# Reordering the streamed weight blocks of a hybrid decoder block on one core

## The chip, the core and the metric

The kernel runs on one core of a Trainium2 chip. Its engines have queues of their own and meet through semaphores: TensorE (PE, with its weight loads shown as PEld), VectorE (DVE), ScalarE (ACT), GpSimd (POOL) and SyncE (SP), which here issues most of the DMAs. The metric is the device time of one execution in microseconds (us), the median of several runs.

## The reference

A decoder block for 256 tokens of width 2048, batch 1, in f32. The input is RMS-normalised and multiplied by one wide matrix `w_in` (2048 x 8760), whose columns feed everything that follows:

- an mLSTM with 4 heads of 256: `mq`, `mk` (through a causal convolution of 4 taps and SiLU), `mv`, the output gate `mo`, the path gate `mz`, input and forget gates `mi`, `mf`;
- native sparse attention with 16 query heads of 64 in 4 key/value groups: queries `nq`, three pairs of keys and values (`kc`,`vc` compressed, `ks`,`vs` selected, `kw`,`vw` windowed), three mixing gates `ng` and a path gate `nz`. The compressed keys and values each go through a small two-layer network with GELU over blocks of 32 tokens.

```python
m_out = hm * jax.nn.sigmoid(mo) * jax.nn.silu(mz)
n_out = n_att * jax.nn.silu(nz)
x = x + jnp.concatenate([m_out, n_out], axis=-1) @ w_out[l]
ple = rmsnorm(p[l] @ ple_proj_w[l], ple_norm_g[l])
x = x + jax.nn.sigmoid(x @ ple_gate_w[l]) * ple
```

A last RMSNorm gives the output.

## The kernel before

All weights are streamed once, in the order of the list `STREAM` (lines 54 to 65). Each entry is a block of columns, cut along the contraction into 216 **units** of mostly 512 KB. Products are made to nearly full f32 precision from rounded parts: ACT rounds a unit to `whi` (L164), DVE takes the remainder `wlo` (L165), and PE multiplies hi by hi, hi by lo and lo by hi. Token-major blocks do this in `mm` at L190 (stationary x, moving weights, two token halves of 128 in two PSUM banks); blocks marked `feat` (the convolved `qk0` to `qk7` and the gates `nz0` to `nz3`) have the weights stationary (L178, L179). Four buffers hold raw, hi and lo units; main results rotate through three PSUM banks (`mainps`), the small transposes through two (`auxps`).

The main loop (L1273 and on) takes one unit per turn, in this order: evacuate the block that ended in the turn before (`evac`, the functions `ev_*`); issue the load of the unit four ahead and the split of the unit three ahead; issue this unit's matmuls; then `advance()`, which runs every **track** by one step. A track is a Python generator: what stands between two `yield`s is issued in one turn, behind that turn's matmuls on PE and behind its split on ACT and DVE. All engines execute in the order of issue. So the place of a step in time is counted in units, and a wait in a step holds all that is queued behind it on its engine.

The tracks that matter here, with their lines:

- `x_squares` (L260) loads x in 8 pieces into `xq`, squares them, and `norm_scale` (L272) makes the token scales `rr` (a power on POOL, L275), `rh`, `rq` and, through PE (L281), the row `rb`. It starts at unit 4.
- `split_w1` (L476) splits the two 1 MB first layers of the compressions; `k_stack` (L364) turns rope'd keys into `kT`.
- `compress` (L485): `cmp_hidden` (L392) for the keys, then for the values. Each is a chain of 14 steps: transposes, copies `kcs`, windows `mov` on POOL, split `movr`, PE matmuls (L430), GELU, second layer. Both use one buffer for `movr`.
- `nsa` (L578): query transposes, scores against the compressed keys, then `cmp_probs` (L624, a softmax over them) beside `attend_all` (L659): 12 sub-steps of four turns each: scores (L670), mask and maximum on DVE (L680, L682), exponentials on ACT (L693), scaling on POOL (L704), transposes on PE (L716), split (L727, L728), product with the values (L740 to L749). It waits for `cmp`, and `attend_all` also for the window keys (`k1`) and the gates (`vw`).
- `conv` (L867): convolution and SiLU of a `qk` block on DVE and ACT (L875 to L882).
- `mlstm` (L903): four heads, three turns each, after `nsa`, `gates` and `conv7`; then normalisation to `hm`.
- `gate_m` (L1012) and `gate_n` (L1050) multiply by the gates and make the hi/lo inputs `mixm`, `mixn` of the output projection; `ple_in` and `ev_ple` make the per-layer embedding.

Blocks before: `cs` (units 0 to 15), `kw`, `vw` (16 to 27), `q0` to `q2` (28 to 51), `qk0` to `qk7` (52 to 83), `mv` (84 to 99), `mo` (100 to 115), `mz` (116 to 131), four times `nz`, `ple` (132 to 151), `out` (152 to 183), `gate` (184 to 215).

## Time and profile before

| | |
|---|---|
| median of 3 runs | 672.66 us (670.83 to 674.17) |
| the profiled execution | 671.72 us, of which the trace spans 670.0 us |
| busy | PE 647.0 us (97%), DVE 456.4 (68%), ACT 376.4 (56%), POOL 73.7 (11%) |
| TensorE's mean granted clock | 0.991 of full speed |
| DMA | 121.05 MB, 181 GB/s on the mean |

Times of the trace count from the span's start. Matmuls are pipelined, and a PE that is shown busy need not be at its peak; here the number of matmuls in a stretch says how far the work got. In the timelines the first number is the start in us, the second the duration; in brackets stands how long the engine was idle before and what ended it.

### The profile page before, as it was taken

To read this page: it belongs to the slowest core of one execution; us is meant where nothing else is said; L and a number is where in the kernel's file an instruction comes from. 1 tells how busy PE (TensorE), PEld (TensorE's weight loads), DVE (VectorE), ACT (ScalarE), POOL (GpSimd) and SP (SyncE) were. 2 spreads that over 40 slices of the span, in tenths; PEclk is the share of its full clock that TensorE was granted. 3 is DMA by queue.
4 is the path that set the end of the run, shared out by engine and by line. 5 is a ranking of instruction groups with operands and counts; after the bars stand their busy time and mean duration, and the time that the engine had idled before them with its cause. 6 is when DMAs were issued, how large, how long until landed. Compare 5 with 4: busy or idle time off the path is not lost. (4 is left out here: it accounts for less than half of the span.)

```text
span 670.0 us, 9336 instructions
## 1 busy us (share of the span) xinstructions
PE 647.0 (97%) x3423; PEld 557.0 (83%) x3423; DVE 456.4 (68%) x682; ACT 376.4 (56%) x643; POOL 73.7 (11%) x78
## 2 busy tenths in 40 slices
PE   8999999999979999999999999997999999999994
PEld 6888999988968888888888888876888888888884
DVE  5667848788789999766675556676645755545564
ACT  5577756477457775665656444566744433445442
POOL 0002303000030112111211000110100000022430
PEclk9999999999999999999999999998999999999998
DMA  8993756565444545555455554453687765566623
GB/s 288 371 355 100 201 167 173 175 198 180 129 121 131 157 156 158 159 157 157 144 164 154 184 155 139 142 149 112 195 297 267 252 183 183 190 184 192 186 97 127
DMA packets 36479, 121.05 MB, mean 181 GB/s; under 512 B 4305, under 2 KB 5073, under 8 KB 35921
## 3 DMA queue, kind: packets, MB, share of 16 engines
q1 hardware_dynamic: 35280, 115.98, 54.7%
q10 hardware_dynamic: 1152, 4.47, 1.8%
q8 instruction: 27, 0.44, 0.3%
q14 instruction: 20, 0.16, 0.1%
HBM read 118.33 MB, written 2.10 MB: 180 GB/s over the span
## 5 line engine op out<-in xcount | busy, mean ns | idle before, releaser
L165 DVE TENSOR_TENSOR wlo<-wraw,whi 128x1024 fp32r<-128x1024 f32 (+3 forms) x218 | 260.3, 1196 | 175.9 <-ACT whi L164 170.2
L164 ACT CAST whi<-wraw 128x1024 fp32r<-128x1024 f32 (+3 forms) x218 | 217.0, 998 | 189.6 <-PE mainps L190 120.9
L190 PE MATMUL mainps<-whi,hT 128*128 128x512 f32 (+3 forms) x768 | 184.0, 360 | 0.9 <-ACT whi L164 0.8
L190 PEld LDWEIGHTS mainps<-whi,hT 128*128 128x128 f32 x768 | 131.7, 189 | 18.1 <-ACT whi L164 1.6
L178 PE MATMUL mainps<-hT,whi 128*128 128x512 f32 x384 | 139.3, 404 | 3.3 <-ACT ple L1091 1.5
L179 PE MATMUL mainps<-hT,wlo 128*128 128x256 f32 x384 | 108.1, 282 | 0.0
L190 PE MATMUL mainps<-wlo,hT 128*128 128x512 f32 (+3 forms) x384 | 106.5, 356 | 0.1
L178 PEld LDWEIGHTS mainps<-hT,whi 128*128 128x128 f32 x384 | 72.9, 190 | 20.7 <-ACT ple L1091 1.8
L190 PEld LDWEIGHTS mainps<-wlo,hT 128*128 128x128 f32 x384 | 68.3, 188 | 9.4 <-DVE wlo L165 0.5
L179 PEld LDWEIGHTS mainps<-hT,wlo 128*128 128x128 f32 x384 | 73.3, 191 | 0.3
L190 PE MATMUL mainps<-whi,x2T 128*128 128x512 f32 (+1 forms) x288 | 70.4, 366 | 0.0
L190 PEld LDWEIGHTS mainps<-whi,x2T 128*128 128x128 f32 x288 | 50.8, 189 | 8.8
L190 PE MATMUL mainps<-wlo,x2T 128*128 128x512 f32 (+1 forms) x144 | 40.9, 366 | 0.0
L704 POOL TENSOR_TENSOR pr<-pr,st 128x1024 f32<-128x1024 f32 x12 | 23.0, 1913 | 143.5 <-DVE st L702 93.3
L190 PE MATMUL mainps<-whi,mixm 128*128 128x512 f32 x128 | 35.5, 399 | 0.0
L190 PE MATMUL mainps<-whi,mixn 128*128 128x512 f32 x128 | 34.2, 389 | 0.0
L878 DVE SCALAR_TENSOR_TENSOR qk<-cv,csb,qk 128x253 f32<-128x253 f32 (+2 forms) x48 | 29.5, 614 | 1.6 <-ACT qk L875 0.2
L190 PEld LDWEIGHTS mainps<-wlo,x2T 128*128 128x128 f32 x144 | 26.0, 189 | 4.4
L190 PEld LDWEIGHTS mainps<-whi,mixn 128*128 128x128 f32 x128 | 24.0, 188 | 5.1
L190 PEld LDWEIGHTS mainps<-whi,mixm 128*128 128x128 f32 x128 | 23.6, 188 | 5.2
L693 ACT ACTIVATE pr<-wideps,st 128x128 f32<-128x128 f32 (+1 forms) x64 | 26.3, 423 | 2.7 <-DVE st L682 2.7
L1191 POOL TENSOR_TENSOR x<-x,gth 128x512 f32<-128x512 f32 x6 | 11.3, 1881 | 117.5 <-PE mainps L190 102.5
(276 smaller groups left out, 711.3 us busy)
## 6 DMA issues: line engine op xcount, KB each, us to landing
wraw<-in_wst_dram SPq DMA_DIRECT2D x183, 512.0 KB, 3.6
wraw<-in_wst_dram SPq DMA_DIRECT2D x24, 344.0 KB, 3.2
wraw<-in_wst_dram SPq DMA_DIRECT2D x8, 304.0 KB, 3.1
xq<-in_x_dram SPq DMA_DIRECT2D x8, 256.0 KB, 9.0
w1raw<-in_w_dram SPq DMA_DIRECT2D x2, 1024.0 KB, 9.9
x<-in_x_dram ACTq DMA_DIRECT2D x4, 512.0 KB, 4.8
out_dram<-x SPq DMA_DIRECT2D x8, 256.0 KB, 2.6
xf<-in_xT_dram SPq DMA_DIRECT2D x3, 512.0 KB, 6.1
```

The costliest lines, as they stand in the source:

```text
L164: A.copy(hi[:, a:z], raw[:, a:z])
L165: V.tensor_tensor(lo[:, a:z], raw[:, a:z], hi[:, a:z].bitcast(F32), OP.subtract)
L178: PE.matmul(o, wh, b.xT(kt, True), start=kt == 0, stop=False, skip_group_check=True)
L179: PE.matmul(o[:, 0], wl, b.xT(kt)[0], start=False, stop=kt == b.nk - 1, skip_group_check=True)
L190: PE.matmul(b.ps[n], xx, (self.hi, self.lo)[part == 2][:, j, a:z], start=kt + part == 0, stop=part == 2 and kt == b.nk - 1)
L693: A.activation(d["pr"][:, j, b], d["ps"][:, j, b], AF.Exp, bias=st[:, 0, j, b:b + 1], accum_out=st[:, 1, j, b:b + 1])
L704: G.tensor_tensor(pf, pf, d["st"][:, 2].rearrange("p j b -> p (j b)")[:, :, None].to_broadcast([128, 2 * jn, nk]), OP.mult)
L878: V.scalar_tensor_tensor(y[:, d:S], a[:, 0:S - d], w(j), y[:, d:S], op0=OP.mult, op1=OP.add)
L1191: G.tensor_tensor(x2[t][:, sl], x2[t][:, sl], ths[t], OP.add)
```

## The change

It reorders `STREAM` and the list of blocks alike: the three query blocks follow `cs`; then `kw`, `vw`; then `mo`, `mv`, and only then the eight convolved blocks; each `ple` block precedes its `nz` block. It lets the compression of the values start four steps behind that of the keys. It moves four POOL multiplications or subtractions to DVE, a second read of PSUM in `ev_mz` from DVE to ACT, and shifts the start of several tracks and steps.

```diff
 STREAM = [("cs", "w_in", span(C_KC, 512) + span(C_KS, 512), KT, 1)]
+STREAM += [(f"q{i}", "w_in", span(C_MI + i * 344, 344), KT, 2) for i in range(3)]
 STREAM += [("kw", "w_in", span(C_KW, 256), KT, 4), ("vw", "w_in", span(C_VW, 304), KT, 2)]
-STREAM += [(f"q{i}", "w_in", span(C_MI + i * 344, 344), KT, 2) for i in range(3)]
+STREAM += [(f"mo{i}", "w_in", span(C_MO + i * 512, 512), KT, 2) for i in range(2)]
+STREAM += [(f"mv{i}", "w_in", span(C_MV + i * 512, 512), KT, 2) for i in range(2)]
 STREAM += [(f"qk{i}", "w_in", span(C_MQ + i * 256, 256), KT, 4) for i in range(8)]
-STREAM += [(f"mv{i}", "w_in", span(C_MV + i * 512, 512), KT, 2) for i in range(2)]
-STREAM += [(f"mo{i}", "w_in", span(C_MO + i * 512, 512), KT, 2) for i in range(2)]
 STREAM += [(f"mz{i}", "w_in", span(C_MZ + i * 512, 512), KT, 2) for i in range(2)]
 for i in range(4):
+    STREAM += [(f"ple{i}", "ple_proj_w", span(i * 512, 512), 2, 2)]
     STREAM += [(f"nz{i}", "w_in", span(C_NZ + i * 256, 256), KT, 4)]
-    STREAM += [(f"ple{i}", "ple_proj_w", span(i * 512, 512), 2, 2)]
...
         V.tensor_scalar(rq, rr, ND ** -0.5, None, op0=OP.mult)
+        yield
+        yield
         ps = aux([128, S])
...
+        while is_v and "ckmm" not in done:
+            yield
         movr = tmp.tile([128, CS, 2, NG, NC16], F32R, name="movr", tag="hm")
...
+        done.add("ckmm")
...
-        yield from cmp_hidden(kcx, pkcol, w1[0], False)
-        yield
-        yield from cmp_hidden(vcx, pvcol, w1[1], True)
+        hk, hv = cmp_hidden(kcx, pkcol, w1[0], False), cmp_hidden(vcx, pvcol, w1[1], True)
+        for _ in range(4):
+            next(hk)
+            yield
+        left = [hk, hv]
+        while left:
+            for h in list(left):
+                if next(h, 1):
+                    left.remove(h)
+            yield
         done.add("cmp")
...
-        G.tensor_tensor(pcf, pcf, a0[:, :, None].to_broadcast([128, T * NH, NC16]), OP.subtract)
+        V.tensor_tensor(pcf, pcf, a0[:, :, None].to_broadcast([128, T * NH, NC16]), OP.subtract)
...
-            G.tensor_tensor(pt, pt, cmul[:, t, None, :].to_broadcast([128, NH, NC16]), OP.mult)
+            V.tensor_tensor(pt, pt, cmul[:, t, None, :].to_broadcast([128, NH, NC16]), OP.mult)
+        yield
...
-        G.tensor_tensor(pcf, pcf, a1[:, :, None].to_broadcast([128, T * NH, NC16]), OP.mult)
+        V.tensor_tensor(pcf, pcf, a1[:, :, None].to_broadcast([128, T * NH, NC16]), OP.mult)
...
             run(s_scale, k - 1)
             run(s_fin, k - 2)
             yield
+            if k == 1:
+                yield
             run(s_max, k)
             run(s_tr, k - 1)
...
         done.add(f"conv{i}")
+        if i == 7:
+            tracks.append(mlstm())
...
-            if i == 1:
-                tracks.append(mlstm())
...
-        while not {"nsa", "gates", "conv7"} <= done:
+        while not {"nsa", "gates"} <= done:
...
                 A.activation(tz, ps[t], AF.Tanh, scale=rh[:, t:t + 1])
-                V.scalar_tensor_tensor(tz, tz, 1.0, ps[t], op0=OP.add, op1=OP.mult)
+                zc = t2([128, 512], name="zc")
+                A.copy(zc, ps[t])
+                V.scalar_tensor_tensor(tz, tz, 1.0, zc, op0=OP.add, op1=OP.mult)
...
         A.activation(th, tz, AF.Tanh, scale=0.5)
+        yield
         V.scalar_tensor_tensor(tz, th, 1.0, tz, op0=OP.add, op1=OP.mult)
-        G.tensor_tensor(tz, tz, natt[:, 2 * i:2 * i + 2], OP.mult)
+        V.tensor_tensor(tz, tz, natt[:, 2 * i:2 * i + 2], OP.mult)
...
-    ple_first = next(i for i, u in enumerate(units) if u.b is mz[1])
+    ple_first = next(i for i, u in enumerate(units) if u.b is mz[0])
...
             if i == 1:
                 nc.sync.dma_start(pos_i, positions)
-            else:
                 tracks.append(x_squares())
```

The list of blocks follows the new `STREAM`: `blocks += mo + mv_b + qk_b + mz`, then `[pb[i], nz[i]]` for each i.

## Rows read from the trace of the kernel before

**Rows 1.** Busy us (instructions) of PE, PEld, DVE, ACT, POOL; then PEclk, DMA, GB/s.
```profile
14.00:51.00 37.00, 37.00 (x164) 30.59 (x163) 24.67 (x44) 25.09 (x45) 0.00 (x0) 1.00 0.97 355
51.00:54.00 3.00, 1.55 (x11) 1.14 (x10) 2.40 (x6) 0.48 (x2) 2.75 (x4) 1.00 0.74 203
...
128.00:133.00 5.00, 4.57 (x30) 4.29 (x29) 4.74 (x12) 4.00 (x8) 0.00 (x0) 1.00 0.67 197
...
180.00:210.00 30.00, 26.46 (x148) 22.90 (x147) 26.91 (x38) 18.37 (x44) 6.46 (x5) 0.94 0.39 119
210.00:262.00 52.00, 52.00 (x293) 44.70 (x292) 50.69 (x76) 36.10 (x75) 5.77 (x3) 1.00 0.48 146
262.00:358.00 96.00, 96.00 (x477) 80.72 (x476) 65.60 (x81) 58.55 (x128) 13.34 (x8) 1.00 0.51 158
...
410.00:440.00 30.00, 29.45 (x162) 25.30 (x160) 20.76 (x43) 17.58 (x30) 3.34 (x2) 1.00 0.46 141
440.00:462.00 22.00, 16.49 (x85) 13.52 (x84) 15.86 (x25) 13.54 (x27) 2.21 (x1) 0.92 0.49 143
...
661.00:670.00 9.00, 0.05 (x1) 0.00 (x0) 2.91 (x10) 1.72 (x3) 0.56 (x1) 0.71 0.63 234
sum 670.00, PE 646.96 PEld 556.99 DVE 456.35 ACT 376.42 POOL 73.66; mean PE 43.13 PEld 37.13 DVE 30.42 ACT 25.09 POOL 4.91
```

**Rows 2.** Waits of PE: waiter, released by: us in total, times, longest us.
```profile
PE auxps L1031 <- DVE mixm L1037: 3.9, 2, 3.1
PE auxps L716 <- POOL pr L704: 2.3, 1, 2.3
PE mainps L178 <- ACT ple L1091: 1.5, 1, 1.5
PE auxps L281 <- POOL rr L275: 1.4, 1, 1.4
PE mainps L178 <- ACT sc L863: 1.2, 1, 1.2
...
PE mainps L178 <- DVE tz L1005: 0.5, 1, 0.5
```

**Rows 3.** Timeline: the twelfth unit's remainder on DVE, PE's pass over it.
```profile
34.93 1.23 DVE L165 TENSOR_TENSOR wlo<-wraw,whi 128x1024 fp32r<-128x1024 f32 x1 [2.82 <-ACT whi L164]
...
38.10 0.39 PE L190 MATMUL mainps<-wlo,hT 128*128 128x512 f32 x1
```

**Rows 4.** Groups by line: DVE from 50 to 72 us, ACT from 53 to 66 us.
```profile
L481 DVE TENSOR_TENSOR w<-w1raw,w 128x512 fp32r<-128x512 f32 x8 | 5.5, 684 | 0.0
...
L507 DVE SCALAR_TENSOR_TENSOR vst<-mainps,rr,vst 128x256 fp32r<-128x256 f32 x2 | 1.0, 480 | 0.9 <-ACT vst L506 0.9
...
L515 ACT ACTIVATE kx<-mainps,rr 128x256 f32<-128x256 f32 x2 | 0.9, 475 | 1.3 <-DVE vst L507 1.3
...
L506 ACT ACTIVATE vst<-mainps,rr 128x256 fp32r<-128x256 f32 x2 | 0.9, 470 | 1.8 <-POOL rr L275 1.8
```

**Rows 5.** Timeline: POOL's first step of the compressed softmax.
```profile
186.92 1.88 POOL L631 TENSOR_TENSOR pc<-pc,cst 128x512 f32<-128x512 f32 x1 [74.93 <-DVE cst L630]
```

**Rows 6.** Timelines of POOL, DVE and PE around two scalings of the attention.
```profile
264.55 1.90 POOL L704 TENSOR_TENSOR pr<-pr,st 128x1024 f32<-128x1024 f32 x1 [11.40 <-PE mainps L190]
...
265.17 2.35 DVE L165 TENSOR_TENSOR wlo<-wraw,whi 128x1024 fp32r<-128x1024 f32 x1
...
221.73 1.90 POOL L704 TENSOR_TENSOR pr<-pr,st 128x1024 f32<-128x1024 f32 x1 [21.20 <-DVE st L702]
...
225.83 1.04 PE L716 MATMUL auxps<-ident,pr 128*128 128x128 f32 x8
```

**Rows 7.** Timeline of ACT and DVE ahead of PE's longest wait, 451 to 454 us.
```profile
451.11 0.62 ACT L1056 CAST mixn<-tz 128x512 fp32r<-128x512 f32 x1 [2.63 <-POOL tz L1054]
...
452.58 0.47 ACT L1036 ACTIVATE mixm<-auxps,csb 128x256 fp32r<-128x256 f32 x1
...
453.85 0.48 DVE L1037 SCALAR_TENSOR_TENSOR mixm<-auxps,csb,mixm 128x256 fp32r<-128x256 f32 x1
```

More of the change, by code (lines that the diff above doesn't have):

```diff
@@ L1235, in hybrid_block @@
     blocks = [Block("cs", ev_cs, h_of, cuts=halves, banks=cs_banks, parts_first=2)]
+    blocks += [Block(f"q{i}", ev_q(i), h_of) for i in range(3)]
     blocks += [Block("kw", ev_kw, h_of), Block("vw", ev_vw, h_of)]
-    blocks += [Block(f"q{i}", ev_q(i), h_of) for i in range(3)]
-    blocks += [Block(f"qk{i}", ev_qk(i), h_of, feat=True) for i in range(8)]
-    blocks += [Block(f"mv{i}", ev_mv(i), h_of) for i in range(2)]
+    mv_b = [Block(f"mv{i}", ev_mv(i), h_of) for i in range(2)]
+    qk_b = [Block(f"qk{i}", ev_qk(i), h_of, feat=True) for i in range(8)]
     pb = [Block(f"ple{i}", ev_ple(i), p_of) for i in range(4)]
@@ L1242, in hybrid_block @@
                   for c, f, n in (("mo", ev_mo, 2), ("mz", ev_mz, 2), ("nz", ev_nz, 4)))
-    blocks += mo + mz
+    blocks += mo + mv_b + qk_b + mz
     for i in range(4):
-        blocks += [nz[i], pb[i]]
+        blocks += [pb[i], nz[i]]
     blocks += [Block(f"out{i}", ev_out(i), mix_of) for i in range(4)]
```

## The prediction

> **What bounds the kernel now.** I read the table of busy times by stretch first, then the waits of PE, then the timelines around those waits. PE is busy 646.96 of 670.0 us [rows 1], and the change neither adds nor drops a matmul: 216 units before and after. So it can win only where PE idles or runs on a slow clock. Of the 23.04 us of idle time, 8.95 lie behind 661 us, after the last matmul [rows 1], and five stretches hold the rest that can move: 1.45 (51 to 54 us), 0.43 (128 to 133), 3.54 (180 to 210), 0.55 (410 to 440) and 5.51 (440 to 462), together 11.48 [rows 1]. The remaining 2.6 belong to the start, which stays. Two of these stretches also show a granted clock of 0.94 over 30 us and of 0.92 over 22 us [rows 1]: the level of 1.2 GHz instead of 2.4 for some microseconds after PE had stood still 2.3 and 3.1 us [rows 2]. That is 0.06 x 30 + 0.08 x 22 = 1.8 + 1.76 us of full-speed work. **The most that a better order can give back is 11.48 + 3.56 = 15.0 us.** The sum below is made against the profiled execution, 671.72 us, which is 0.94 below the median of 672.66 and inside the runs' spread.
>
> **The change part by part.** A step's place is counted in units by its yields; I counted both orders from the code.
>
> *Token scales.* PE waited 1.4 us for the power on POOL [rows 2]. `x_squares` now starts three units earlier and its matmul comes two steps later, so `rr` is there before it is wanted: 1.45 us go. `rb` comes later, but its first reader is 70 units away. In exchange three of the eight x pieces (3 x 256 KB = 0.79 MB) go ahead of weights in SP's queue, in a stretch where DMA is 97% busy at 355 GB/s [rows 1]: weights of units 8 to 13 land up to 2.2 us later. The tightest of them is the twelfth unit: its remainder ends at 36.16 us and PE's pass over it starts at 38.10 [rows 3], 1.94 us of slack. Loss between 0 and 2.2; I take 0.3, what the slack fails to cover.
>
> *Query blocks second.* A 512-column matmul takes 37.00 us / 164 = 226 ns [rows 1], so I estimate 152 ns for 344 columns and 0.9 us for a query unit's first token half (six matmuls). The second half needs a bank of `cs`, which the chain `vst`, its remainder, `kx` frees after 0.47 + 0.48 + 0.48 = 1.43 us [rows 4]. In the old place the first half was longer. I take 0.5 (0 to 1.5). The query units then last 1.8 us, and units 16 to 22 each carry 0.68 us of DVE for the split of the first layers [rows 4] beside the key stack, so the lead of three units shrinks: 0.4 (0 to 1.5).
>
> *Compressions overlapped.* The chain for the values starts at unit 27 instead of 37 and `cmp` is done at 41 instead of 50. It waits for the keys' `ckmm` without cost, as the keys' matmuls come at unit 30 and the values' split at 32. The attention now waits for the window keys (unit 51) and the gates (54): its first scores come at unit 55 instead of 65, it ends at 114 instead of 124. The wait of 0.43 at 128 us, DVE's end of that chain, can occur for each of two chains: 0.4 (0 to 0.9).
>
> *Compressed softmax on DVE, one step more.* POOL took 1.88 us for the first subtraction [rows 5] with ACT's exponential queued behind it and behind that the evacuation `sc` for which PE waited 1.2; then PE waited 2.3 for the first scaling L704 [rows 2]. DVE now does this in short steps, in the `mo` blocks, where there is no convolution: the stretch most like it, attention beside `mv` and `mo`, has DVE busy 65.6 of 96 us and PE idle for none [rows 1]. The extra yield gives the first scaling one more unit. The 3.54 and 1.8 go; I leave 0.3 (0 to 3.5).
>
> *Convolution under attention.* Before, half of the `qk` blocks ran beside the attention; now all eight do (units 84 to 115, attention to 113). There DVE is busy 50.69 of 52 us, 97.5%, with PE idle for 0 [rows 1]. It just holds, and must hold twice as long. A scaling ends at 223.63 us and PE transposes its result at 225.83 [rows 6], 2.2 us of slack. I take 0.7 (0 up to the second rival). A remainder that met a scaling of 1.90 us on POOL took 2.35 us, against 1.23 alone [rows 6, 3]; the 97.5% contain this already. The Trainium skill has a rule for it that speaks against this order ("SBUF — State Buffer", section "Who interferes with whom"): a DVE instruction with two SBUF inputs and a GpSimd instruction that reads SBUF shut each other out for a whole instruction. The trace agrees (2.35 beside 1.90); by that rule at its hardest, with nothing hidden, seven scalings in the convolved blocks would make the sum 7 x 1.9 = 13.3 us worse.
>
> *mLSTM and `mz`.* The mLSTM is released by the last convolution, at unit 119 instead of 124. The extra copy moves the second read of the bank to ACT, and PE no longer waits for DVE's L1005 (0.5 [rows 2]), but ACT now needs two instructions a half and still has mLSTM exponentials ahead of them: I leave 0.8 (0 to 1.5).
>
> *Gates and mixing.* PE's longest waits, 3.1 and 0.8 for `mixm` and 1.5 for the `ple` evacuation [rows 2], came when ACT stood 2.63 us behind POOL's multiplication by `natt` [rows 7] and DVE behind ACT. That multiplication goes to DVE and the step is cut in two. What stays: the four second transposes of two tracks need two banks that the first ones hold. In that unit ACT has a split (1.0) and four evacuations of 0.47, DVE 1.23 and four of 0.48 [rows 7, 3], so the first bank is free at about 1.0 + 1.1 + 1.2 + 1.0 = 4.3 us, when PE arrives at 0.9 + 2.8 = 3.7, and the second 0.5 later than wanted: 1.1. With 0.6 for the `ple` evacuation, 1.7 stay of 5.51 + 1.76 = 7.3 (0 to 7.3).
>
> *At no cost:* `mo` and `mv` earlier (evacuated by ACT alone), `ple_in` eight units earlier (an ACT-queue load with 12 units to land), and `nz3` last: its `mixn` is ready at unit 154 and first used at 159; the x loads behind it go out from 155 and are first read at 160. If one of these were late, a unit of the output projection would wait, about 3 us.
>
> **Sum:** 0.3 + 0.5 + 0.4 + 0.4 + 0.3 + 0.7 + 0.8 + 1.7 = 5.1 us stay or are new; 15.0 - 5.1 = 9.9 us are won. 671.72 - 9.9 = **661.8 us**, 1.6% below the median of before.
>
> **The rivals.** *The mixing stretch does not get better.* Both tracks still start in the same turn, and the mLSTM's own tail on DVE, POOL and ACT is unchanged; then up to 7.3 instead of 1.7 + 0.8 stay: 661.8 + 4.8 = 666.6. Against it: ACT's 2.63 us behind POOL were the head of that wait [rows 7].
> *DVE falls short in the convolved blocks.* Each of the seven scalings there costs DVE 2.35 - 1.23 = 1.12 us [rows 6, 3]. If the 2.5% of DVE that are left [rows 1] do not cover this over eight blocks, PE waits for it: 7 x 1.12 = 7.8, 669.6 us, no change that can be told. Against it: PE idles for none in 52 us of this mixture, three scalings among them [rows 1]. This is the mechanism of the rule of the Trainium skill named above ("SBUF — State Buffer").
> *Each scaling in the convolved blocks stalls PE (slower than before).* If DVE's queue delays L704 by more than the 2.2 us of slack [rows 6], PE stands before the transposes as it did at the first scaling: 2.3 us plus 1.8 of clock, for seven sub-steps 28.7, so 661.8 + 28 = 690 us. In the new order the scaling falls in the third unit of a block, away from the evacuation and the first convolution step, which speaks against it.
> *The earlier compression buys nothing* because the attention is held by keys and gates: true in part and counted; it has no price of its own.
>
> **How the numbers follow.** Forecast 0.62; mixing as before 0.20; DVE short 0.11; scalings that stall 0.07. The forecast's own range goes from all 15.0 won (656.7) to its upper ends at the front and in `mz` together (about 665). The range of 656 to 668 adds the first rival and leaves out the second, the third and strays, 2 in 10. A measurement of this kernel can tell some 0.5% from no change, 3.4 us: faster means below 669.3, which the forecast and the first rival give, and a little of the second: 0.84. Same 0.10, slower 0.06.
>
> **What would show it.** Right: no wait of PE at L281, L716 or L1031 above 1 us, a granted clock of 1.00 in every stretch behind the start, first attention scores before 150 us, the mLSTM's first matmuls some 20 us earlier (13.6 us of five units and 7 of waits), DVE above 95% in the convolved blocks with PE idle near 0. Wrong: PE waits on L716 for L704 in several blocks; PE waits for `wlo` within the first 50 us; a wait of 3 us at L1031 and a slow clock behind it; a lead that vanishes in the query units.

## The result, and the profile after

The changed kernel takes **668.31 us** (median of 11 runs, 667.21 to 670.60) against 672.66 (11 runs): ratio 0.994, interval 0.9927 to 0.9954. It is faster by 0.6%: 4.35 us where 10.9 were forecast, just outside the range of 656 to 668. Its profiled execution took 668.31 us, of which the trace spans 666.6: 3.4 less than before. Lines below about 280 keep their numbers; L281, L704, L716, L1031, L1036, L1037, L1052 of before are L283, L717, L729, L1048, L1053, L1054, L1069 now.

PE's waits in the changed kernel, to be read against [rows 2]:

```profile
PE auxps L1048 <- DVE mixm L1054: 3.0, 2, 2.5
PE auxps L383 <- DVE kst L372: 1.8, 1, 1.8
...
PE auxps L729 <- POOL pr L717: 1.3, 1, 1.3
PE mainps L190 <- ACT kx L527: 1.1, 1, 1.1
...
PE auxps L434 <- DVE movr L428: 0.5, 1, 0.5
PE mainps L190 <- ACT zc L1021: 0.3, 1, 0.3
```

Gone are POOL's `rr` (1.4), the first scaling (2.3) and the evacuation `sc` (1.2). New are the wait for the key parts `kst` (1.8), for a bank of the first block, freed by `kx` (1.1), and for one of the attention's later scalings, `pr` (1.3). The wait for `mixm` has hardly moved: 3.9 before, 3.0 now.

Busy times by stretch of the changed kernel, columns as in [rows 1]:

```profile
0.00:17.00 17.00, 13.05 (x52) 10.07 (x53) 8.18 (x25) 8.84 (x14) 0.70 (x6) 1.00 0.84 285
...
52.00:56.00 4.00, 2.87 (x17) 2.46 (x16) 2.85 (x6) 1.95 (x6) 0.00 (x0) 1.00 0.83 240
...
61.00:65.00 4.00, 2.07 (x14) 1.65 (x14) 3.96 (x8) 4.00 (x7) 0.00 (x0) 1.00 0.46 150
...
80.00:100.00 20.00, 19.54 (x135) 18.75 (x134) 16.77 (x38) 11.10 (x20) 7.36 (x14) 1.00 0.57 168
...
180.00:262.00 82.00, 82.00 (x418) 69.36 (x417) 50.72 (x66) 47.38 (x101) 11.43 (x7) 1.00 0.50 155
262.00:330.00 68.00, 68.00 (x408) 59.82 (x407) 66.00 (x100) 48.94 (x104) 7.87 (x4) 1.00 0.44 140
330.00:380.00 50.00, 48.66 (x263) 41.69 (x261) 41.77 (x63) 29.27 (x40) 2.18 (x1) 1.00 0.61 185
380.00:426.00 46.00, 45.66 (x220) 38.19 (x219) 29.04 (x57) 24.72 (x41) 2.04 (x1) 1.00 0.44 137
426.00:450.00 24.00, 20.74 (x112) 17.34 (x111) 18.16 (x27) 15.55 (x29) 0.00 (x0) 0.93 0.47 142
```

The attention's start (180 to 262 us) is full, as forecast. The idle time behind 17 us is 1.13 + 1.93 + 0.46 + 1.34 + 0.34 + 3.26 = 8.46 us, and the clock of 0.93 over 24 us (part of it at 1.2 GHz instead of 2.4) costs 1.7: 10.1 where 15.0 stood before and 4.8 were forecast (the 5.1 without the start's 0.3). The start idles 3.95 us, 1.34 more than before, which makes 15.0 - 10.1 - 1.3 = 3.6, the 3.4 of the spans. Nothing ties that 1.34 to the change: in the nine kernels below with the same code up to 80 us the start idles 1.6 to 3.3 us, on both sides of the 2.61 of before.

Two parts came out otherwise; the timelines show where. The front, ACT and VectorE:

```profile
52.44 0.47 ACT L518 ACTIVATE vst<-mainps,rr 128x256 fp32r<-128x256 f32 x1
...
54.40 0.47 ACT L527 ACTIVATE kx<-mainps,rr 128x256 f32<-128x256 f32 x1 [1.50 <-DVE vst L519]
...
57.59 0.79 ACT L164 CAST whi<-wraw 128x688 fp32r<-128x688 f32 x1
...
58.41 0.88 DVE L165 TENSOR_TENSOR wlo<-wraw,whi 128x688 fp32r<-128x688 f32 x1 [2.65 <-ACT whi L164]
...
62.79 1.22 DVE L372 TENSOR_TENSOR kst<-kx,kst 128x1024 fp32r<-128x1024 f32 x1
```

ACT empties the first block's banks from 52.44 to 57.59 us (1.50 us of it standing for VectorE's remainder `vst`, which is queued behind the remainders of two units, the row `rb` and a split piece) and rounds no unit meanwhile, so VectorE in turn stands 2.65 us; the rotation and the remainders queue behind that, and `kst` ends at 64.0 with PE waiting. The mixing:

```profile
428.07 1.29 DVE L1039 TENSOR_TENSOR hm<-hm,gmt 128x512 f32<-128x512 f32 x2
...
430.41 1.28 DVE L1039 TENSOR_TENSOR hm<-hm,gmt 128x512 f32<-128x512 f32 x2
431.60 1.03 PE L1048 MATMUL auxps<-ident,hm 128*128 128x128 f32 x8
...
433.19 0.63 ACT L1069 ACTIVATE th<-tz 128x512 f32<-128x512 f32 x1 [2.64 <-DVE tz L880]
...
437.41 0.84 ACT L1053 ACTIVATE mixm<-auxps,csb 128x256 fp32r<-128x256 f32 x2 [1.31 <-DVE mixm L1054]
...
438.55 0.99 PE L1048 MATMUL auxps<-ident,hm 128*128 128x128 f32 x4 [2.53 <-DVE mixm L1054]
```

"x2" and "x8": both halves of the mixing (one of each `mz` block) run in the same turns, and their transposes take both spare banks at once. ACT stands 2.64 us, as before, but ahead of the `tanh` (L1069), not behind a multiplication by `natt`.

### The profile page after: what moved, and what is told of

It is laid out like the page before. It is cut to its first block, busy times and chain, and to the rows that moved or that the text cites. A ratio compares the mean times of both kernels' runs of the same rounds, so it can differ in the third digit from the quotient of the medians.

```text
span 666.6 us, 9325 instructions
## 1 busy us (share of the span) xinstructions
PE 645.2 (97%) x3423; PEld 555.6 (83%) x3423; DVE 456.0 (68%) x690; ACT 378.6 (57%) x647; POOL 62.6 (9%) x70
## 4 chain that ended last, share of the span: by engine, by line
PE 84%; DVE 8%; ACT 3%; issue 2%; DMA 1%; POOL 1%; SPq 0%; ACTq 0%; POOLq 0%
PE mainps L190 56%; PE mainps L178 10%; PE mainps L179 5%; DVE wlo L165 3%; PE wideps L190 3%; PE wideps L683 2%; PE auxps L729 1%; ACT whi L164 1%; DMA wraw<-in_wst_dram 1%; PE wideps L958 1%; PE po L762 1%; PE po L760 1%; PE auxps L1185 1%; PE auxps L933 1%; PE wideps L622 1%
## 5 line engine op out<-in xcount | busy, mean ns | idle before, releaser
L178 PE MATMUL mainps<-hT,whi 128*128 128x512 f32 x384 | 137.6, 400 | 0.3 <-ACT ple L1109 0.3
L717 POOL TENSOR_TENSOR pr<-pr,st 128x1024 f32<-128x1024 f32 x12 | 23.3, 1944 | 219.1 <-DVE st L715 219.1
L878 ACT COPY sc<-mainps 128x512 f32<-128x512 f32 x24 | 14.1, 586 | 17.5 <-PE mainps L179 17.4
L893 DVE SCALAR_TENSOR_TENSOR qk<-cv,csb,qk 128x253 f32<-128x253 f32 (+2 forms) x48 | 23.1, 481 | 1.1
```

What stands on the lines that cost most here:

```text
L178: PE.matmul(o, wh, b.xT(kt, True), start=kt == 0, stop=False, skip_group_check=True)
L717: G.tensor_tensor(pf, pf, d["st"][:, 2].rearrange("p j b -> p (j b)")[:, :, None].to_broadcast([128, 2 * jn, nk]), OP.mult)
L878: A.copy(sc, ps[m])
L893: V.scalar_tensor_tensor(y[:, d:S], a[:, 0:S - d], w(j), y[:, d:S], op0=OP.mult, op1=OP.add)
```

## The experiments

Each is the changed kernel with the edit shown, unless it says otherwise. Times are medians of 5 to 12 runs; the kernel before, run beside them, had medians of 671.39 to 672.86 us, so kernels of different groups are compared by their ratios to it (with 95% intervals; they are no quotients of the medians). Two kernels whose intervals overlap can't be told apart by time. Where the order of the blocks is edited, the diff shows the list of blocks; `STREAM` follows it.

**The mixing: banks, the tanh, POOL.** `mix_gap` puts a turn between the two pairs of transposes:

```diff
                 V.scalar_tensor_tensor(lo, ps[:, j], g, hi.bitcast(F32), op0=OP.mult, op1=OP.subtract)
+            if k0 == 4 * i:
+                yield
```

> The second pair of transposes of each mixing track is put one turn behind the evacuation of the first pair. Theory A (the 2.5 us stall at the second transposes comes from taking both spare banks again in the turn in which they are still being emptied): the wait of PE at the transposes for mixm falls from 3.0 us to under 0.6, the granted clock stays near 1.0 over 428-449 us, the time falls by 3 to 4.7 us against the changed kernel, to 663.6-665.3. Rival B (ACT and VectorE are late as a whole there, because ACT stands 2.64 us at the tanh of the gate for VectorE): the stall only moves to the banks of the projection and gate blocks, the sum of PE's waits in 426-450 falls by less than 1 us, the time is within 1 us of 668.3.

666.64 us, 0.991 (0.9884 to 0.9935). The wait at the transposes fell to 0.7 (A: under 0.6) and the clock stayed 1.00, as A said; but 1.5 us came up at an evacuation of the gate blocks (L878), as B said. Half of each; by time it can't be told from the changed kernel.

`th_late` issues the gate's tanh a turn later:

```diff
+        yield
         th = t2([128, 2, S], name="th")
```

> The tanh of every gate block is issued one turn later, so that ACT is not held 2.64 us for VectorE's two additions ahead of it. Theory B (this hold of ACT is the head of the mixing wait): ACT's wait at the tanh falls from 2.64 to under 0.8 us, PE's wait at the transposes from 3.0 to about 1, the slow clock behind it goes, the time falls by 2.5 to 4 us, to 664.3-665.8. Rival A (the reuse of the two spare banks within one turn is enough by itself): ACT's wait falls all the same but PE still waits 2 us or more there, the time is within 1 us of 668.3.

667.05 us, 0.9916 (0.9887 to 0.9945), again not told from it by time. The wait fell from 3.0 to 2.3, the clock stayed slow: the hold of ACT is a part, not the head. `natt_pool` undoes one edit, VectorE's multiplication by `natt`:

```diff
-        V.tensor_tensor(tz, tz, natt[:, 2 * i:2 * i + 2], OP.mult)
+        G.tensor_tensor(tz, tz, natt[:, 2 * i:2 * i + 2], OP.mult)
```

> Of the change only one edit is undone: the multiplication of the gate by the attention output goes back from VectorE to POOL. The forecast's step (ACT's 2.63 us of waiting behind POOL's multiplication was the head of the mixing wait, and taking it off POOL saves 3 us or more): the time rises by 2.5 to 5 us, to 670.8-673.3, PE's waits in 426-450 grow by 2 us. Rival (ACT is held ahead of that, at the tanh, for VectorE, so where the multiplication runs does not matter): the time is within 1 us of 668.3.

669.27 us, 0.995 (0.9932 to 0.9968), the wait at the transposes 3.1: no difference that can be told. In the changed kernel the multiplication is not the head of the mixing wait, as the forecast had it. `mix_all` joins the first two and issues of each pair both high parts, then both low parts:

```diff
+            for j in range(2):
+                A.activation(mixm[:, 0, k0 + j], ps[:, j], AF.Copy, scale=mgcol[:, k0 + j:k0 + j + 1])
             for j in range(2):
...
-                A.activation(hi, ps[:, j], AF.Copy, scale=g)
```

> Three edits of the mixing at once: a turn between the two pairs of transposes, the tanh of the gate block one turn later, and of each pair both high parts first, then both low parts (instead of high, low, high, low, where ACT waited 1.31 and 0.58 us for VectorE's low part). Theory A+B (bank reuse and the two hold-ups of ACT are all that stalls PE here): PE's waits over 426-455 fall from 5.0 us (3.0 for mixm, the rest for evacuations) to under 1.2, granted clock 1.0; the time falls by 3.5 to 5 us, to 663.3-664.8. Rival E (each of the two engines has more work in these turns than the turns are long, so a stall left out in one place comes back at the next bank): waits of 2 us or more stay, the time is 666 to 667, as with either edit alone.

663.81 us, 0.9858 (0.9833 to 0.9884). By stretch, PE is now full where it idled 3.26 us, at full clock:

```profile
426.00:450.00 24.00, 24.00 (x137) 20.80 (x136) 20.68 (x30) 19.32 (x34) 0.00 (x0) 1.00 0.61 196
```

So the stall can be taken away there; what the order of the evacuations gives alone was not tried. Why the changed kernel runs into it, the next group shows.

**The place of the convolved blocks.** `conv_first` undoes that part of the order:

```diff
-    blocks += mo + mv_b + qk_b + mz
+    blocks += qk_b + mv_b + mo + mz
```

> Of the change one part is undone: the convolved blocks go back ahead of the values and the output gate (first block, query, key, value, convolved, values, gate). Theory F (it was this edit that freed the attention's start, by taking the convolution's multiply-adds off VectorE there): PE idles 2.5 us or more in the attention's first 60 us again and loses up to 1.8 us to a slow clock, while the single 1.3 us stall at the probabilities late in the attention goes: 670 to 672. Rival G (the query block's place and the earlier probabilities are enough, VectorE's load may lie anywhere under the attention): within 1 us of 668.3.

667.56 us, 0.9912 (0.9888 to 0.9935): the time does not tell it from the changed kernel, so G held, but not for its reason. By stretch, the attention's start idles 2.9 us again, with VectorE at 80.41 of 82, though at other waits than before: 1.8 us for `pcT` and four scalings in a row that come 0.3 to 0.6 us late each (228 to 272 us), without a slow clock. The mixing idles none:

```profile
180.00:262.00 82.00, 79.08 (x460) 68.10 (x461) 80.41 (x118) 55.51 (x118) 10.05 (x5) 1.00 0.46 148
...
426.00:450.00 24.00, 24.00 (x137) 20.70 (x136) 18.07 (x26) 17.00 (x31) 0.00 (x0) 1.00 0.54 162
```

```profile
PE auxps L729 <- POOL pr L717: 1.8, 4, 0.6
```

and in VectorE's timeline the halves of the mixing lie 13 us apart, each alone ("x1"):

```profile
416.35 0.68 DVE L1039 TENSOR_TENSOR hm<-hm,gmt 128x512 f32<-128x512 f32 x1
...
429.45 0.68 DVE L1039 TENSOR_TENSOR hm<-hm,gmt 128x512 f32<-128x512 f32 x1
```

So this part of the change moved a loss from the attention's start to the mixing; over 100 to 450 us idle time and slow clock are 4.0 us in `conv_first` and 6.6 in the changed kernel. The groups of the tiles `natt` (the attention's sums) and `em` (the mLSTM's first step of each head), with the durations (min/median/max) and the first and last start, say how. In the changed kernel, shown first, the mLSTM's first head comes 27.2 us after the attention's last sum (345.2 to 372.4), where before, shown below it, it was 14.2 (372.6 to 386.8), and in `conv_first` 14.1:

```profile
L772 DVE TENSOR_TENSOR natt<-po,ot x16: 407/414/419, 189.0 to 345.2; 64x256 f32<-64x256 f32 x16
...
L943 DVE TENSOR_TENSOR em<-auxps,mask_t x4: 417/418/418, 372.4 to 407.3; 128x256 f32<-128x256 f32 x4
```

```profile
L759 DVE TENSOR_TENSOR natt<-po,ot x16: 408/413/419, 221.5 to 372.6; 64x256 f32<-64x256 f32 x16
...
L928 DVE TENSOR_TENSOR em<-auxps,mask_t x4: 416/418/418, 386.8 to 422.3; 128x256 f32<-128x256 f32 x4
```

`conv_mixed` puts the value blocks between the convolved ones, the last convolved block staying last:

```diff
-    blocks += mo + mv_b + qk_b + mz
+    blocks += mo + qk_b[0:3] + mv_b[0:1] + qk_b[3:6] + mv_b[1:2] + qk_b[6:8] + mz
```

> The two value blocks are put between the convolved blocks (gate, gate, three convolved, value, three convolved, value, two convolved), so that the multiply-adds of the convolution spread over 83 turns' length less densely. Theory K (VectorE is short by some 0.2 us a turn while eight convolved blocks follow each other under the attention, 97% busy over 262-330 us, and the stall of 1.3 us at the probabilities is the end of that): that stall goes, PE idles under 0.3 us over 180-380, VectorE's busiest 68 us fall below 90%; 666.6 to 667.4. Rival L (the stall is one meeting of POOL's multiplication with a low part on VectorE, whatever the load): a stall of 1 us or more comes back at another probability; within 0.6 us of 668.3.

666.64 us, 0.9911 (0.988 to 0.9943). PE idles 0.06 us over 180 to 380 and VectorE's busy time over 262 to 330 falls to 60.22 of 68, as K says. The mixing's wait stays at 3.3 us, its mLSTM starting at 371.9, and by time it can't be told from the changed kernel. Then the two that settle it. `mv_last`:

```diff
-    blocks += mo + mv_b + qk_b + mz
+    blocks += mo + qk_b[0:4] + mv_b[0:1] + qk_b[4:8] + mv_b[1:2] + mz
```

> The changed kernel with the second value block moved behind the convolved blocks (gate, gate, four convolved, value, four convolved, value), so that the last convolution is over some 13 us earlier. Theory O (the mLSTM of the changed kernel starts 27 us after the attention's last sum, where 14 would do, because its own part of the change put the convolved blocks last; it then ends after the second gate block, and both halves of the mixing are released into the same turns): the mLSTM's first row moves from 372 to about 360 us, the halves' multiplications by the gate lie 8 us or more apart instead of side by side, PE's wait at the mixing's transposes (3.0 us) and the slow clock behind it go, and with the convolution thinned the 1.3 us stall at the probabilities goes as well: 662 to 664.5. Rival A' (the two spare banks are too few for a half of the mixing alone): the wait at the transposes stays 1.5 us or more: 665.5 to 667.

663.41 us, 0.9877 (0.9862 to 0.9892). PE's waits no longer list the mixing, the mLSTM's first head starts at 358.6, and in VectorE's timeline the halves are apart (the group of `em` stands below it):

```profile
411.48 0.69 DVE L1040 TENSOR_TENSOR hm<-hm,gmt 128x512 f32<-128x512 f32 x1
...
424.58 0.68 DVE L1040 TENSOR_TENSOR hm<-hm,gmt 128x512 f32<-128x512 f32 x1
```

```profile
L944 DVE TENSOR_TENSOR em<-auxps,mask_t x4: 415/417/418, 358.6 to 394.5; 128x256 f32<-128x256 f32 x4
```

One part of the expectation missed: VectorE's busy time over 262 to 330 us is as low as in `conv_mixed` (58.80 of 68), and yet PE waits for a scaling twice, 0.57 us at 265 and 0.70 at 336, each time at the third scaling beside four convolved blocks in a row (the account of the prediction says why):

```profile
PE auxps L730 <- POOL pr L718: 1.3, 2, 0.7
```

`mix_apart`:

```diff
-        while "mlstm" not in done:
+        while "mlstm" not in done or (i and "mix0" not in done):
             yield
```

> The changed kernel with one condition more: the second half of the mixing waits until the first half is done. Everything else stays, the order high, low, high, low too. Theory O: with the halves apart each takes one spare bank a turn, the wait at the transposes falls from 3.0 to under 0.6 us and the clock stays 1.00: 663.3 to 665.3. Rival A' (the hold of ACT at the tanh and the order of the evacuations stall PE even for one half): 1.5 us or more of waits stay in 426-450: 666 to 667.5.

664.36 us, 0.9884 (0.9866 to 0.9901). PE is busy 23.35 of 24 us in the mixing, at full clock, and its wait at the transposes is this:

```profile
PE auxps L1048 <- DVE hm L1039: 0.6, 1, 0.6
```

Both held in the mixing: the halves' meeting makes the stall, and in the changed kernel the place of the last convolved block makes the meeting.

`cmp_pool` puts the four operations of the compressed probabilities back on POOL:

```diff
-        V.tensor_tensor(pcf, pcf, a0[:, :, None].to_broadcast([128, T * NH, NC16]), OP.subtract)
+        G.tensor_tensor(pcf, pcf, a0[:, :, None].to_broadcast([128, T * NH, NC16]), OP.subtract)
...
```

> Of the change one part is undone: the four multiplications and subtractions of the compressed probabilities go back from VectorE to POOL. Theory H (they were part of the stall of 3.5 us and of the slow clock at the attention's start): PE idles 1 to 3 us there again, 669.3 to 672. Rival (with the gates and values ahead, the compressed probabilities have time enough on either engine): within 0.8 us of 668.3.

669.67 us, 0.9945 (0.9924 to 0.9966), and PE is busy 82.00 of 82 us at the attention's start: not told from the changed kernel. With the convolution out of the way, POOL does as well.

**The front.** `split_late` starts the split of the compression weights seven turns later, `split_early` three turns earlier with two pieces a turn, `split_mid` at turn 20 with two pieces a turn:

```diff
-        elif i == KT - 1:
-            tracks.append(split_w1(w1r))
...
+        if i == KT + 6:
+            tracks.append(split_w1(w1r))
```

(`i == 12` in `split_early`, `i == KT + 4` in `split_mid`; these two also yield only after every second piece.)

> The split of the two compression weights into high and low parts begins 7 turns later, behind the key block's evacuation. Theory C (the splits that stand in ACT's and VectorE's queues between the query block's evacuation and the key block's high and low parts hold up both): PE's wait at the transposes of the key parts falls from 1.8 to under 0.5 us, that for the query block's last bank from 1.1 to about 0.5, the time falls by 1.5 to 2.5 us, to 665.8-666.8. Rival D (ACT's evacuations of the query and key blocks and VectorE's rotation are long enough alone): the two waits together stay over 2 us, the time is within 0.8 us of 668.3.

672.08 us, 0.999 (0.9973 to 1.0007): C's two waits did go, but PE waited for the compression's moving parts instead, and the clock fell behind it (0.83 over 20 us, 3.4 us). PE's waits, and the stretch:

```profile
PE auxps L434 <- DVE movr L428: 4.1, 2, 3.6
```

```profile
80.00:100.00 20.00, 15.95 (x91) 14.77 (x90) 16.20 (x33) 9.79 (x18) 6.76 (x11) 0.83 0.45 132
```

> The split of the two compression weights begins 3 turns earlier and takes two pieces a turn, so that it is over when the first block's banks are emptied (turns 12 to 15, where VectorE was 66% and ACT 65% busy). Theory C (what the front lost is the splits standing between the evacuation of the first blocks and the key parts; the compression's tail has room only if they come no later): PE's wait for kst falls from 1.8 to under 0.6 us, the wait for the first block's bank from 1.1 to about 0.5, the wait for movr stays at 0.5, no slow clock over 61-80 us; the time falls by 2.5 to 4.5 us, to 663.8-665.8. Rival D (ACT's evacuations alone hold the key parts up, or the splits now delay the high and low parts of the first 16 turns): PE idles 1 us or more in 17-52 or the two waits stay over 2 us; 667.5 or more.

672.44 us, 0.9991 (0.9975 to 1.0007). The wait for `kst` went, that for the bank became 4.6, and the clock fell behind it (0.57 over 56 to 61 us, 0.68 over 61 to 65: 3.4 us). VectorE's free third of 17 to 52 us (23.07 of 35 us busy in the changed kernel) lies ahead of 44 us, where units come late; behind that it has no gap, and the pieces push the evacuation back. VectorE's timeline, then PE's waits:

```profile
43.70 1.23 DVE L165 TENSOR_TENSOR wlo<-wraw,whi 128x1024 fp32r<-128x1024 f32 x1 [2.45 <-ACT whi L164]
...
56.94 0.48 DVE L520 SCALAR_TENSOR_TENSOR vst<-mainps,rr,vst 128x256 fp32r<-128x256 f32 x1
```

```profile
PE mainps L190 <- ACT kx L528: 4.6, 1, 4.6
```

> The split of the two compression weights goes into turns 20 to 23, two pieces a turn: behind the first block's evacuation and behind the key parts, but ahead of the turns over 80-90 us where VectorE has no room (16.8 of 20 us busy) and where a later split delayed the compression's moving parts. Theory C' (both waits of the front come from the pieces that stand ahead of the evacuation and of the key parts, and there is one gap, 65 to 76 us, where VectorE idles 3.7 us with the pieces in it): the wait for kst falls from 1.8 to under 0.5 us, the wait for movr stays under 1, the clock stays 1.00 over 61-100; the time falls by 2 to 4 us, to 664.3-666.3. Rival D' (there is no room anywhere in the front; each place only moves the stall): the waits for kst, movr and the transposes of the compression keep a sum of 2.3 us or more; 667.5 or more.

666.17 us, 0.9903 (0.9872 to 0.9933). `kst` 1.0 instead of 1.8, `movr` 0.7, the bank still 1.1, the clock 1.00. The time is the low end of C', but its wait for `kst` (under 0.5) was missed, and its interval overlaps the changed kernel's a little.

`b_q2` is the kernel *before* with the query block second and nothing else:

```diff
 blocks = [Block("cs", ev_cs, h_of, cuts=halves, banks=cs_banks, parts_first=2)]
+blocks += [Block(f"q{i}", ev_q(i), h_of) for i in range(3)]
 blocks += [Block("kw", ev_kw, h_of), Block("vw", ev_vw, h_of)]
-blocks += [Block(f"q{i}", ev_q(i), h_of) for i in range(3)]
```

> The kernel before with one part of the change alone: the query block second. Theory M: the stall at the key parts appears (1.5 to 2.2 us), with 0.5 to 1.3 us at the first block's bank beside the wait of 1.4 us that the kernel before has there, and up to 1.6 us of slow clock; the attention still starts behind the compression and gains nothing: 673.5 to 677. Rival N: the front looks as in the kernel before, 670.5 to 673.

675.97 us, 1.0057 (1.0037 to 1.0076): slower than before. Its waits of PE hold the 1.8 for `kst` (at the line of before), and a larger one that no theory named: at 136 us the window values' banks were freed 4.9 us late, because the rotation of the queries, the key stack and this evacuation had come into the same turns of VectorE; behind it the clock was 0.96 over the 80 us from 100 on, 3.2 us:

```profile
PE mainps L178 <- DVE gates L541: 4.9, 1, 4.9
...
PE auxps L381 <- DVE kst L370: 1.8, 1, 1.8
```

`kw_q_vw` puts the window keys' four turns ahead of the query block again:

```diff
+    blocks += [Block("kw", ev_kw, h_of)]
     blocks += [Block(f"q{i}", ev_q(i), h_of) for i in range(3)]
-    blocks += [Block("kw", ev_kw, h_of), Block("vw", ev_vw, h_of)]
+    blocks += [Block("vw", ev_vw, h_of)]
```

> The changed kernel with the first key block of the window moved back ahead of the query block (first block, key, query, value, gate, values, convolved). Theory M (the front's new stalls come from the length of a turn: a query turn gives PE 1.88 us, a key turn 2.88, so the first four turns after the first block last 7.5 us instead of 11.5, and ACT's evacuations, the rotation and the splits don't fit): with the key block's four turns back, the waits for the bank and for kst fall from 1.1 and 1.8 us to under 0.5 together, the clock stays 1.00 over 56-80 us, and since the compression sets when the attention starts, nothing is lost later; 663.8 to 666. Rival N (the front's work is late because of what it is, the pieces of the split and the order of evacuation): waits of 2 us or more stay, 667.3 or more.

668.64 us, 0.9944 (0.993 to 0.9957): neither theory whole. The wait for `kst` is gone, as M says, but the time and the sum of the waits are N's. PE's waits show 2.2 us at the first block's bank and 1.1 at the moving parts in its place, and the clock fell to 0.72 over 56 to 61 us. So the short turns make the wait for `kst`, and the front as a whole does not gain by that alone:

```profile
PE mainps L191 <- ACT kx L528: 2.2, 1, 2.2
...
PE auxps L435 <- DVE movr L429: 1.1, 1, 1.1
```

`rr_undo` starts the squares three turns later again and takes out the two turns ahead of the scales' broadcast:

```diff
         V.tensor_scalar(rq, rr, ND ** -0.5, None, op0=OP.mult)
-        yield
-        yield
...
                 nc.sync.dma_start(pos_i, positions)
+            else:
                 tracks.append(x_squares())
```

> The changed kernel with the sums of squares three turns later and without the two turns before the broadcast of the scales, as before. If that part of the change is what removed the 1.45 us wait at 51 us, as forecast, the wait comes back (1.2 to 1.6 us) and the stall at the key parts stays near 1.8 or grows: 669 to 671. Rival (with the query block second the banks of the first block are late anyway, so that the wait only changes its name): within 0.7 us of 668.3.

668.79 us, 0.9949 (0.9932 to 0.9967). The wait for `rr` is back, that for the bank is not in the list, and the time can't be told from the changed kernel's: the wait only changes its name.

```profile
PE auxps L281 <- POOL rr L275: 1.4, 1, 1.4
```

**All together.** `best_a` is `mix_all` with `split_mid`, `best_b` has `conv_mixed` besides, and `best_d` the order of `kw_q_vw` as well.

> The three mixing edits and the split in turns 20 to 23 together. If the two stalls are independent, as theories A+B and C' have it, their gains add: 4.5 us (measured) and 2 to 4 us, 660 to 662. If the split's place gives nothing (rival D'), 663.0 to 664.5.

> The same with the value blocks between the convolved blocks. If all three are independent: 659 to 661, idle of PE between 17 and 657 us under 2 us. If theory K fails, as the run before it; if the spread convolution delays the mLSTM and the mixing: 1 us or more above it.

> The three mixing edits, the split in turns 20 to 23, the value blocks between the convolved ones, and the key block ahead of the query block. If theory M holds beside the others: 657 to 659, PE idle under 2 us between 17 and 657 us. If the four long turns alone had been enough, the late split costs again at the compression's moving parts (0.5 to 1.5 us): 659 to 661.

Measured: 659.46, 659.57 and 659.18 us; 0.9805 (0.9773 to 0.9837), 0.9805 (0.9777 to 0.9833), 0.9803 (0.9789 to 0.9816). All three beat both kernels, by some 13 and 9 us, and can't be told from each other. The gains of the mixing and of the split are consistent with adding; a third edit on top does not show. In `best_d`, beside two waits in the first 8 us, one wait above 0.5 us is left, at the compression's moving parts, as the second reading of its expectation said:

```profile
PE auxps L436 <- DVE movr L430: 1.1, 1, 1.1
```

## Where the prediction was right and where it failed

Of the 5.3 us by which the 10.1 exceed the 4.8 that were forecast, 3.2 lie in the mixing, 2.2 in the front and 0.6 in the convolution under the attention; the rest came out 0.7 better.

**Right.** The attention's first sum comes 32.5 us earlier (221.5 to 189.0), the start of the attention is full at full clock (0.3 forecast), the wait for `mz` is 0.34 (0.8 forecast). Of the two reasons given for the full start, the one that counts is that no convolution is there (`conv_first`); that VectorE does the compressed softmax made no difference that can be told (`cmp_pool`). The compression's 0.46 us against 0.4 is luck: the wait foreseen, for `gl` at the end of a chain, is gone, and PE waits for `movr` at its beginning instead (88.6 us). Two signs named for it being right were missed by a little: the first attention scores come at 155.7 us, not before 150, and the mLSTM's first matmul 14.3 us earlier (384.7 to 370.4), not 20, since most of the waits it was to gain came back as new ones ahead of it. Of the rivals the first, the mixing as before at 666.6 us, came nearest in what happened; the number of the second, 669.6, lies even nearer, by chance: its mechanism came, at 1.3 us instead of 7.8.

**Mixing: forecast 1.7, measured 3.26 idle + 1.7 of slow clock = 5.0.** The step that failed is the count of banks in *Gates and mixing*: first bank free at 4.3 us, PE there at 3.7, once ACT no longer stands behind POOL's multiplication. Counted from the first transposes at 431.60, PE was there after 4.4 us (436.02) and had its bank after 6.9 (438.55). The count has a split and four evacuations on ACT; ACT stood for VectorE all the same, until 433.19, ahead of the tanh, and then did the tanh, two `ple` evacuations and the split before it began the first bank at 435.62. `natt_pool` shows that where the multiplication runs does not matter here. And that both halves ask for the banks in one turn was taken as given, though the change itself sets it: moving the convolved blocks last holds the mLSTM back by 27.2 - 14.2 = 13 us behind an attention that ends 27.4 us earlier, so it ends behind the second `mz` block again, and both halves are let go in the same turns. The count also left out the handing to and fro of ACT and VectorE between four evacuations, in which ACT waits 1.31 and 0.58 us. The first rival's words "Both tracks still start in the same turn" were the cause; it was given 0.20, and what sets that turn was not asked. `mv_last` and `mix_apart` show it from both sides. The wait of 3 us at the transposes with a slow clock behind it is the prediction's own sign of being wrong.

**Front: forecast 0.5 + 0.4, measured 1.13 + 1.93, and 1.7 of slow clock in eight of ten profiles.** The bank's term took the chain `vst`, remainder, `kx` as 1.43 us; it took 2.43 (52.44 to 54.87), since ACT stood 1.50 for the remainder. The step that the query units of 1.8 us shrink the lead of three units, 0.4, had the mechanism and mis-sized it. It charged VectorE's split pieces to the lead, and left out that ACT's evacuations stop the rounding for 5.2 us (52.44 to 57.59); before they did so for 4.5 (52.84 to 57.29), but the four turns beside them were 11.5 us long instead of 7.5. `b_q2` brings the wait for `kst` into the kernel before by that edit alone, `kw_q_vw` takes it out. The 1.45 us at `rr` were counted as won; `rr_undo` shows that the bank's wait had taken their place. In the ten kernels with the same front the bank is free 2.4 us after ACT's first evacuation; what sets how far ACT is behind PE then, and with it the bank's wait, is open: 0 to 1.4 us in the ten, 2.2 in `kw_q_vw`, none in `best_d`.

**Convolution under the attention: forecast 0.7, measured 1.34, one stall.** It is the second rival's mechanism, VectorE falling short in the convolved blocks, and PE pays for it before the transposes of a scaled tile. The timelines of POOL, VectorE and PE in the changed kernel show the last scaling before the convolution begins to load VectorE and the last scaling of all.

```profile
244.58 1.89 POOL L717 TENSOR_TENSOR pr<-pr,st 128x1024 f32<-128x1024 f32 x1 [11.96 <-DVE st L715]
...
249.65 1.03 PE L729 MATMUL auxps<-ident,pr 128*128 128x128 f32 x8
...
332.78 2.18 POOL L717 TENSOR_TENSOR pr<-pr,st 128x1024 f32<-128x1024 f32 x1 [12.86 <-DVE st L715]
...
333.12 2.92 DVE L165 TENSOR_TENSOR wlo<-wraw,whi 128x1024 fp32r<-128x1024 f32 x1
...
335.01 1.09 PE L729 MATMUL auxps<-ident,pr 128*128 128x128 f32 x8 [1.33 <-POOL pr L717]
```

From the end of a scaling to PE's transposes of its result there are 2.8 to 3.2 us at the five from 194.23 to 249.65 us, then 2.7, 2.3, 1.6, 0.9 and 0.2; at the last PE stands 1.3. From 244.58 on the scalings, released by VectorE, come every 14.4 to 15.0 us, PE's transposes every 14.0 to 14.3. So "It just holds" was a misreading: in the 52 us that it rests on PE idled for none, but the slack fell there too, from 2.2 us to 1.7 and 0.8 (225.83, 240.10 and 253.95 us in the kernel before). In `conv_first` the slack is used up by 213 us, and the next four scalings stall PE; with four convolved blocks in a row (`mv_last`) it gives out at the third scaling of each four, by 0.57 and 0.70 us; with three (`conv_mixed`) the least that is left is 0.05, and PE does not wait.

The last remainder takes 1.23 us alone and 2.92 here: 1.7 more, nearly the 1.8 that the scaling still had to run. For this meeting the Trainium skill's rule holds as the page states it ("SBUF — State Buffer", section "Who interferes with whom": VectorE with two SBUF inputs and GpSimd shut each other out for an instruction). The 13.3 us that the prediction set for seven such meetings did not come. The last five scalings each met an instruction of VectorE and lengthened it, by 5.9 us in all (0.69 to 1.82 us three times, 1.23 to 2.09 and to 2.92); that is more than the 4.5 us by which VectorE fell behind PE, and 3.2 of these were slack.

**The edits, priced.** Convolved blocks last: the attention's start won, the mixing lost, no net gain that can be told (`conv_first`). Query block second: a loss taken alone (`b_q2`), most of it at the window values' banks, where the changed kernel does not wait. Compressed probabilities and `natt` on VectorE, and the earlier scales: nothing that can be told. The gain of 4.35 us belongs to no one part that was tried; the overlap of the two compressions, the extra copy in `ev_mz` and the added turns of the attention and of the gate were not undone alone.

## What to carry to other kernels

When work is moved earlier, ask for every later track which condition releases it after the move: here an edit that freed one stage put the last input of the next one at the end of the list, and the time won was spent waiting for it. Two tracks that are let go by one event meet in the same turns and ask for the same few banks; keeping them apart costs one condition and was worth 4 us here. And mean busy shares don't say where work fits: an engine that was 66% busy over 35 us had no gap in the last seven of them. Nor does a stretch without waits show that it holds: take the time from a producer's end to its reader, step by step, and see whether it shrinks.

## What was not expected of the hardware

Ten kernels share all code up to 80 us, and in the profile of each PE waits 1.8 us for `kst`. In eight of these profiles TensorE's granted clock is below full over 61 to 80 us behind that wait, in those of the changed kernel and of `mix_all` it stays 1.00. By stretch, `mix_gap`:

```profile
61.00:65.00 4.00, 2.07 (x14) 1.93 (x14) 4.00 (x6) 4.00 (x8) 0.00 (x0) 0.95 0.30 88
65.00:80.00 15.00, 15.00 (x95) 14.89 (x95) 9.81 (x17) 11.19 (x23) 2.56 (x6) 0.90 0.58 166
```

That is 0.05 x 4 + 0.10 x 15 = 1.7 us of full-speed work lost to the lower level, 1.2 GHz instead of 2.4; the other seven give 1.6 to 1.8. So the same stall cost 2 us in two profiles and nearly 4 in eight, and a single profile shows one of the two. The changed kernel's own profile shows the cheaper one.
